# The first mixer's share of the second block's output projection, moved in among the other mixers

## The chip, the cores and the metric

The kernel runs as one launch on one core of a Trainium2 chip. The metric is the device time of that launch in microseconds, the median of three runs.

## The reference

Two blocks follow each other on the same 512 x 1024 tensor x, all in float32. The change touches only the second block, which has two layers. One layer computes:

```
h = rms_norm(x, norm_g[l, 0]) * (1 + sc1) + sh1
aq, ak, av, bq, bff, bfb, bi, bg, cq, ck, cv = split(h @ w_in[l])
o_a = mixer_a(aq, ak, av)            # full attention, 6 heads of 64: 384 columns
o_b = mixer_b(bq, bff, bfb, bi, bg)  # gated linear scan, both directions, 4 heads: 256 columns
o_c = mixer_c(cq, ck, cv)            # attention with a fixed bias, 6 heads: 384 columns
x = x + g1 * (concat(o_a, o_b, o_c) @ w_out[l])
h = rms_norm(x, norm_g[l, 1]) * (1 + sc2) + sh2
x = x + g2 * conv_ffn(h)
```

`w_out` is 1024 x 1024. Its first 384 rows meet o_a alone, so that part of the product needs only mixer a.

## The kernel before, in words

Everything is held transposed: tiles of 128 features by 512 positions. A float32 product is made of three matmuls in a rounded format (`mm3`, line 178): every operand is split into a high and a low part (`hi`, a ScalarE cast, line 141; `lo`, a VectorE subtraction, line 146), and high times high, low times high and high times low are summed in PSUM. `wload` (line 151) brings a weight tile in: a DMA into one of two raw buffers, one cast for up to 1024 columns, one subtraction per 512 columns, into one of two pairs wh, wl.

A layer of block 2 (`block2`, line 1728) writes x to DRAM (xd, eight tiles of 128 x 512), runs the mixers, reloads x, and does the output projection in eight tiles n (`residual`, line 1719: matmuls into a PSUM tile dn, then one VectorE instruction x = dn * gate + x). Each tile has 8 feature steps k of three matmuls. The tiles n = 0 to 2 are done for all 512 columns at once, n = 3 to 7 first for columns 0 to 255 and later for 256 to 511. In between stands the first half of the norm in front of the FFN (`norm_halves`): squares, their sum, a column sum on TensorE, a reciprocal root on GpSimd, rows on TensorE, then the scaled halves hh and hl. The FFN's first matmuls (up) use that first half.

The mixers are Python generators, each yielding a cost at the end of a step. `weave` (line 1617) takes several such streams with a weight each and always continues the one with the smallest cost divided by weight. The third weave of a layer has three streams: mixer b's second head pair (four projections, then `b_levels`, its scan by nine doubling distances, then output and norm); the twelve half-heads of mixer c (`c_units`, line 1425); and a chain of mixer b's first output, two `c_prep` (line 1392: a projection, its norm and the split of the queries that later heads of c need), norms, two gate projections (`b_gate`) and `room`. `room` (line 1285) sends the mixers' finished outputs through `mix_done` (line 1275), which splits them into tiles oh, ol. These stand in a pool of 24 buffers (`hblk`, line 511), which hold the projections' input hh, hl (16 of them) and the attention tiles E as well.

The order in which the generators emit is a priority, not the final order: the framework's scheduler simulates the engines and puts into each engine's queue, among what is ready, what was emitted first. Each engine, and SP's queue of DMA issues, then runs its queue strictly in that order. PSUM tiles of the tag mm (three banks) serve the projections, the levels and dn.

Of the kernel before, what the change touches and what calls it, by code (L numbers as in the profile page):

```python
# [13 lines left out]
ALU = mybir.AluOpType  # L14
AX = mybir.AxisListType

P = 128
D = 1024
KD = D // P
S = 512  # L20
# [83 lines left out]
class Kern:  # L104
# [1527 lines left out]
                s[2] += c  # L1632
                held = []

    def mixers(self):
        nc = self.nc
        self.gn = self.cp.tile([P, 1], F32, tag="gb2", name=self.nm("gb2"))
        nc.sync.dma_start(self.gn, self.A["gb_2"][self.l])
        self.gc = self.cp.tile([P, 2], F32, tag="gc2", name=self.nm("gc2"))
        nc.sync.dma_start(self.gc, self.A["gc_2"][self.l])  # L1640
        nc.vector.tensor_scalar(self.gc[:, 0:1], self.gc[:, 0:1], 0.125, None, op0=ALU.mult)
        self.cqs, self.cks = [], []
        self.full, self.wait = True, []
        self.oh, self.ol, self.y2, self.bz, self.cn, self.bst, self.bav = {}, {}, {}, {}, {}, {}, {}
        self.zz = [self.bp.tile([P, 2, S], F32, tag="zz", name=self.nm("zz"), bufs=2) for _ in range(2)]
        for z in self.zz:
            nc.gpsimd.memset(z[64:P, 0], 0.0)
            nc.gpsimd.memset(z[0:64, 1], 0.0)
        self.weave((self.b_prep(0), 8.0), (self.a_prep(), 25.5))
        self.weave((self.b_levels(0), 7.0), (self.a_units(), 31), (self.stagger(self.c_prep([3]), self.c_prep([0]), self.c_vals()), 20.0))  # L1650
        if 1:
            for i in (0, 1, 2):
                self.mix_done(i, self.y2[i])
            self.weave((self.chain(self.b_prep(1), self.b_levels(1), self.b_out(1), self.b_norm(1)), 40.0), (self.c_units(), 22.0),
                       (self.chain(self.b_out(0), self.stagger(self.c_prep([1]), self.b_norm(0), self.c_prep([2]), self.b_gate(1), self.b_gate(0)), self.room()), 28.0))
            self.b_done(0)
            self.b_done(1)

# [69 lines left out]
    def block2(self):  # L1728
        nc, tc, A, F = self.nc, self.tc, self.A, self.fill
        self.stat, self.ptb, self.halves = [("s", 2), ("pt", 2)], 2, 0  # L1730
        self.psum = lambda tn, name="mm": self.ps1(name)
        self.bw = {"t": S}
        self.cp = self.ctx.enter_context(tc.tile_pool(name="cp2", bufs=1, reuse_waits="tile"))
        self.ind64 = self.const("ind64", [P, 2])
        self.lmask = self.const("lmask", [P, 5, 32]).bitcast(I32)

        lbr = self.const("b_lb", [P, 2, 2, 2])
        e = self.cp.tile([P, 3, 2, 2, 2], F32, tag="lbe", name="lbe")[:, 0]
        mx = self.cp.tile([P, 2, 2], F32, tag="lbm", name="lbm")
        nc.vector.tensor_tensor(mx, lbr[:, :, 0, :], lbr[:, :, 1, :], op=ALU.max)  # L1740
        for l in range(2):
            nc.vector.tensor_tensor(e[:, :, l, :], lbr[:, :, l, :], mx, op=ALU.subtract)
        nc.scalar.activation(e, e, AF.Exp)
        nc.vector.tensor_tensor(mx, e[:, :, 0, :], e[:, :, 1, :], op=ALU.add)
        rc = self.cp.tile([P, 2, 2], F32, tag="lbr", name="lbr")
        nc.vector.reciprocal(rc, mx)
        self.lb = self.cp.tile([P, 2, 2, 2], F32, tag="lb", name="lb")
        self.oml = self.cp.tile([P, 2, 2, 2], F32, tag="oml", name="oml")
        for l in range(2):
            nc.vector.tensor_tensor(e[:, :, l, :], e[:, :, l, :], rc, op=ALU.mult)  # L1750
        nc.vector.tensor_tensor(self.lb[:, :, 0, :], e[:, :, 0, :], e[:, :, 0, :], op=ALU.subtract)
        nc.vector.tensor_tensor(mx, e[:, :, 0, :], e[:, :, 1, :], op=ALU.add)
        nc.vector.tensor_tensor(self.lb[:, :, 1, :], mx, e[:, :, 0, :], op=ALU.subtract)
        nc.vector.tensor_scalar(self.oml, self.lb, -1.0, 1.0, op0=ALU.mult, op1=ALU.add)
        self.g1 = self.gains("ng1", A["norm_g_2"][1, 0])
        for l in range(2):
            self.l = l
            with ExitStack() as lay:
                g2 = self.gains("ng2", A["norm_g_2"][l, 1])
                mod = self.ada[l][0]  # L1760
                xd = self.dram([KD, P, S], f"xm{l}")
                with self.pool(f"bq{l}", bufs=1, side="right") as bq, self.pool(f"bpm{l}", bufs=1) as bp:
                    self.bp = self.ptp = Pools(bp, bq, 'f2,t,rot,va2,qa,bz,pT'.split(","))
                    self.bb = dict(t=4, rx=1, rot=4, qa=6, ka=6, y=7, bz=2, f=1, yz=2, ex=2)
                    for n in range(KD):
                        nc.sync.dma_start(xd[n], self.x[n])
                    self.mixers()
                    bq.tile([P, 56], F32, tag="pad", name=f"pad{l}")
                    oy = [self.oh[i] for i in range(8)], [self.ol[i] for i in range(8)]
                    self.x = []  # L1770
                    self.x = []
                    for n in range(KD):
                        x = self.hblk(F32, "x")
                        nc.sync.dma_start(x, xd[n])
                        self.x.append(x)
                    ks = [(k, k) for k in (0, 1, 2, 5, 6, 3, 4, 7)]
                    late = []
                    for n in range(KD):
                        w = self.wload(A["w_out_2"][l, n], KD, P)
                        if n < KD - 5:  # L1780
                            self.residual(n, [(w, oy, ks)], (0, S), mod[:, 16 + n, 0:1])
                        else:
                            self.residual(n, [(w, oy, ks)], (0, 256), mod[:, 16 + n, 0:1])
                            late.append(w)
                with tc.tile_pool(name=f"bpf{l}", bufs=1, reuse_waits="tile") as self.bp:
                    self.bb = dict(t=5, act=44, mw=2, w3=2)
                    parts = self.norm_halves(mod, g2, 3, 4, lambda: self.b2("act"))
                    F.add(next(parts))
                    F.drain()
                    for n in [*range(KD - 2, KD), *range(KD - 5, KD - 2)]:  # L1790
                        w = late[n - KD + 5] if n >= KD - 2 else self.wload(A["w_out_2"][l, n], KD, P)
                        self.residual(n, [(w, oy, ks)], (256, S), mod[:, 16 + n, 0:1])
                    F.add(next(parts))
                    F.drain()
                    self.halves = 2
                    self.ffn(mod)
        for n in range(KD):
            nc.sync.dma_start(A["outT"][n], self.x[n])
# [114 lines left out]
```

## Time and profile before

| | |
|---|---|
| median of 3 runs | 3018.26 us (3018.15 to 3021.32) |
| the profiled execution | 3018.07 us, span 3016.3 us |
| TensorE busy | 2910.5 us, 96% of the span |
| VectorE busy | 1921.0 us, 64% |
| ScalarE busy | 1351.2 us, 45% |
| GpSimd busy | 249.8 us, 8% |
| DMA through SP's queue | 328.81 MB, 32.9% of 16 engines' span |

Times in the profile are microseconds from the start of the span. PE is TensorE's matmuls, PEld its weight loads, DVE is VectorE, ACT is ScalarE, POOL is GpSimd, SPq is SP's queue of DMA issues. A matmul's busy time is a modelled one and overlaps that of the next; its pace is read from start to start. PEclk is the granted TensorE clock as a share of 2.4 GHz; the levels are 2.4 and 1.2 GHz, so a value between is a mixture over time. An arrow in square brackets says how long an engine had stood idle before an instruction, and what ended that.

### The profile page before, as it was taken

To read this page: it belongs to the slowest core of one execution; us is meant where nothing else is said; L and a number is where in the kernel's file an instruction comes from. 1 tells how busy PE (TensorE), PEld (TensorE's weight loads), DVE (VectorE), ACT (ScalarE), POOL (GpSimd) and SP (SyncE) were. 2 spreads that over 40 slices of the span, in tenths; PEclk is the share of its full clock that TensorE was granted. 3 is DMA by queue.
4 is the path that set the end of the run, shared out by engine and by line. 5 is a ranking of instruction groups with operands and counts; after the bars stand their busy time and mean duration, and the time that the engine had idled before them with its cause. 6 is when DMAs were issued, how large, how long until landed. Compare 5 with 4: busy or idle time off the path is not lost.

```text
span 3016.3 us, 46253 instructions
## 1 busy us (share of the span) xinstructions
PE 2910.5 (96%) x17942; PEld 2415.4 (80%) x17942; DVE 1921.0 (64%) x3731; ACT 1351.2 (45%) x2417; POOL 249.8 (8%) x492
## 2 busy tenths in 40 slices
PE   7999999999998999999999999999999998999999
PEld 5888888888887888777778776788888876788887
DVE  5565655555556566665666777688853788576642
ACT  3445454322235345653225675544433676454421
POOL 0000000001112000000112222000000223000000
PEclk9999999999998999999999998999999999999999
DMA  6221111333342323124664211355543311232233
GB/s 228 87 67 60 48 63 64 121 127 120 119 161 84 125 83 107 52 69 169 222 216 134 70 50 47 99 175 196 203 144 109 103 43 60 79 105 98 98 102 95
DMA packets 113164, 331.77 MB, mean 110 GB/s; under 512 B 18160, under 2 KB 20720, under 8 KB 112944
## 3 DMA queue, kind: packets, MB, share of 16 engines
q1 hardware_dynamic: 112944, 328.81, 32.9%
q8 instruction: 141, 2.31, 0.3%
q14 instruction: 79, 0.65, 0.1%
HBM read 300.51 MB, written 17.76 MB: 106 GB/s over the span
## 4 chain that ended last, share of the span: by engine, by line
PE 83%; DVE 8%; ACT 2%; issue 1%; DMA 1%; POOL 1%; SPq 0%; DVEq 0%; ACTq 0%; POOLq 0%
PE mm L186 31%; PE up L186 15%; PE dn L186 10%; PE pu L186 5%; PE pv L600 4%; PE pt L595 4%; PE po L186 3%; PE s L907 2%; PE pre L186 1%; PE s L624 1%; PE s L1267 1%; DVE zz L1571 1%; DVE wl L146 1%; PE pq L186 1%; DVE E L607 1%
## 5 line engine op out<-in xcount | busy, mean ns | idle before, releaser
L146 DVE TENSOR_TENSOR wl<-wraw,wh 128x512 fp32r<-128x512 f32 x704 | 472.4, 710 | 389.2 <-ACT wh L141 385.7
L141 ACT CAST wh<-wraw 128x1024 fp32r<-128x1024 f32 (+4 forms) x363 | 364.9, 1005 | 741.0 <-PE mm L186 227.4
L186 PE MATMUL mm<-hh,wh 128*128 128x512 f32 (+1 forms) x1232 | 483.5, 396 | 11.1 <-ACT wh L141 4.0
L186 PE MATMUL mm<-hl,wh 128*128 128x512 f32 (+1 forms) x1232 | 486.1, 395 | 0.0
L186 PE MATMUL mm<-hh,wl 128*128 128x512 f32 (+1 forms) x1232 | 484.9, 394 | 0.2
L186 PEld LDWEIGHTS mm<-hh,wh 128*128 128x128 f32 x1232 | 233.5, 191 | 59.8 <-ACT wh L141 6.7
L186 PEld LDWEIGHTS mm<-hh,wl 128*128 128x128 f32 x1232 | 234.4, 190 | 49.3 <-DVE wl L146 3.0
L186 PEld LDWEIGHTS mm<-hl,wh 128*128 128x128 f32 x1232 | 234.8, 191 | 46.8 <-issue 2.9
L186 PE MATMUL up<-hh,wh 128*128 128x512 f32 (+1 forms) x688 | 260.8, 381 | 3.4 <-ACT wh L141 2.1
L186 PE MATMUL up<-hh,wl 128*128 128x512 f32 (+1 forms) x688 | 261.1, 380 | 0.2 <-DVE wl L146 0.2
L186 PE MATMUL up<-hl,wh 128*128 128x512 f32 (+1 forms) x688 | 260.7, 380 | 0.5 <-DVE hl L352 0.2
L597 ACT COPY pT<-pt 128x512 f32<-128x512 f32 (+1 forms) x304 | 158.8, 551 | 176.6 <-PE pt L595 175.3
L283 DVE SCALAR_TENSOR_TENSOR macc<-mw,sc,macc 128x1024 f32<-128x1024 f32 x140 | 181.7, 1313 | 70.7 <-DMA mw<-w_mod 37.5
L595 PE MATMUL pt<-ident,E 128*128 128x128 f32 x1120 | 174.6, 282 | 4.7 <-DVE E L607 4.2
L595 PEld LDWEIGHTS pt<-ident,E 128*128 128x128 f32 x1120 | 127.2, 141 | 37.3 <-issue 25.7
L186 PEld LDWEIGHTS up<-hh,wh 128*128 128x128 f32 x688 | 128.9, 188 | 29.1 <-ACT wh L141 2.5
L186 PEld LDWEIGHTS up<-hl,wh 128*128 128x128 f32 x688 | 129.1, 188 | 26.3 <-DVE hl L352 1.1
L186 PEld LDWEIGHTS up<-hh,wl 128*128 128x128 f32 x688 | 129.2, 188 | 25.5 <-issue 0.8
L1020 POOL TENSOR_TENSOR m<-m,gt 128x768 f32<-128x768 f32 (+1 forms) x32 | 55.1, 1721 | 1084.3 <-DVE gt L1016 755.6
L186 PE MATMUL mm<-ch,wh 128*128 128x256 f32 x496 | 141.8, 286 | 0.1
L186 PE MATMUL mm<-ch,wl 128*128 128x256 f32 x496 | 141.6, 286 | 0.0
L186 PE MATMUL mm<-cl,wh 128*128 128x256 f32 x496 | 141.3, 285 | 0.0
(442 smaller groups left out, 6129.6 us busy)
## 6 DMA issues: line engine op xcount, KB each, us to landing
wraw<-w_in SPq DMA_DIRECT2D x158, 512.0 KB, 3.5
mw<-w_ada SPq DMA_DIRECT2D x96, 512.0 KB, 4.3
wraw<-w_up SPq DMA_DIRECT2D x88, 512.0 KB, 3.5
mw<-w_mod SPq DMA_DIRECT2D x32, 512.0 KB, 3.6
wraw<-w_down SPq DMA_DIRECT2D x32, 512.0 KB, 3.5
wraw<-w_branch SPq DMA_DIRECT2D x24, 512.0 KB, 4.0
wraw<-w_out SPq DMA_DIRECT2D x22, 512.0 KB, 3.4
wraw<-w_o SPq DMA_DIRECT2D x19, 512.0 KB, 4.2
```

Source lines behind the costliest of these rows:

```text
L141: self.nc.scalar.copy(out, in_)
L146: (eng or self.nc.vector).tensor_tensor(out, in_, hi.bitcast(F32), op=ALU.subtract)
L186: self.last = self.nc.tensor.matmul(ps[: n1 - n0, c0 - o:c1 - o], lhsT=a[:, k, n0:n1], rhs=b[j][:, c0:c1], start=start and i == 0, stop=st ...
L283: nc.vector.scalar_tensor_tensor(acc[r], w, sc[:, k, r:r + 1], acc[r], op0=ALU.mult, op1=ALU.add)
L595: nc.tensor.transpose(pt[:, o * P:o * P + P], ecol(j, kb), self.ident)
L597: nc.scalar.copy(tt[:, :n], pt[:, :n])
L600: nc.tensor.matmul(pv[64 * j:64 * j + 64, :P], lhsT=vst(kb), rhs=tt[:, o * P:o * P + P], start=i == ends[j][0], stop=i == ends[j][-1])
L607: self.nc.vector.tensor_scalar(e, e, r, None, op0=ALU.mult)
L624: nc.tensor.matmul(s[:, c0:c1], lhsT=q[:, i * P:(i + 1) * P], rhs=kp[:, a0:a0 + c1 - c0], start=pi == 0, stop=pi == 1)
L907: self.nc.tensor.matmul(ps, lhsT=a[:96, i * P:(i + 1) * P], rhs=b[:96, c0:c1], start=pi == 0, stop=pi == 2)
L1020: nc.gpsimd.tensor_tensor(ms[n][:, :tn], ms[n][:, :tn], m[:, :tn], op=ALU.add)
L1267: nc.tensor.matmul(s, lhsT=q[:, i * P:(i + 1) * P], rhs=kp, start=pi == 0, stop=pi == 1)
```

## The change

A new generator, `w_out_a`, computes for each of the eight tiles n the part of the output projection that belongs to mixer a (k = 0, 1, 2), multiplies it by the gate, adds it to that tile of x from DRAM and writes the tile back. It is emitted at the end of the third stream, behind `room`, and that stream's weight goes from 28 to 45. The projection behind the mixers then covers the five other steps, in the order 5, 6, 3, 4, 7, with weight tiles of 640 columns instead of 1024.

```
+    def w_out_a(self, xd, mod):
+        nc = self.nc
+        oy = [self.oh[i] for i in range(3)], [self.ol[i] for i in range(3)]
+        for n in range(KD):
+            x = self.b2("t", name="xa")
+            nc.sync.dma_start(x, xd[n])
+            w = self.wload(self.A["w_out_2"][self.l, n][:, :3 * P], 3, P)
+            ps = self.ps1("dn")
+            self.mm3(ps, w, oy, [(0, S)])
+            nc.vector.scalar_tensor_tensor(x, ps, mod[:, 16 + n, 0:1], x, op0=ALU.mult, op1=ALU.add)
+            nc.sync.dma_start(xd[n], x)
+            yield 2.1
+
-    def mixers(self):
+    def mixers(self, xd, mod):
...
-                       (self.chain(self.b_out(0), self.stagger(self.c_prep([1]), self.b_norm(0), self.c_prep([2]), self.b_gate(1), self.b_gate(0)), self.room()), 28.0))
+                       (self.chain(self.b_out(0), self.stagger(self.c_prep([1]), self.b_norm(0), self.c_prep([2]), self.b_gate(1), self.b_gate(0)), self.room(), self.w_out_a(xd, mod)), 45.0))
...
-                    ks = [(k, k) for k in (0, 1, 2, 5, 6, 3, 4, 7)]
+                    ks = [(k - 3, k) for k in (5, 6, 3, 4, 7)]
...
-                        w = self.wload(A["w_out_2"][l, n], KD, P)
+                        w = self.wload(A["w_out_2"][l, n][:, 3 * P:], 5, P)
...
-                        w = late[n - KD + 5] if n >= KD - 2 else self.wload(A["w_out_2"][l, n], KD, P)
+                        w = late[n - KD + 5] if n >= KD - 2 else self.wload(A["w_out_2"][l, n][:, 3 * P:], 5, P)
```

## Rows read from the trace of the kernel before

**Rows 1.** The page: busy time of the engines over the span.
```profile
PE 2910.5 (96%) x17942; PEld 2415.4 (80%) x17942; DVE 1921.0 (64%) x3731; ACT 1351.2 (45%) x2417; POOL 249.8 (8%) x492
```

**Rows 2.** Table by stage, layer 0: length, busy us by engine, clock, DMA share, GB/s.
```profile
1776.00:1818.00 42.00, 42.00 (x266) 33.92 (x266) 26.63 (x65) 32.78 (x52) 3.44 (x3) 1.00 0.25 76
1818.00:1882.00 64.00, 58.64 (x525) 42.36 (x524) 51.14 (x122) 36.65 (x78) 22.18 (x43) 0.84 0.14 46
1882.00:1920.00 38.00, 33.74 (x250) 24.24 (x249) 23.95 (x66) 20.62 (x43) 3.05 (x11) 1.00 0.24 73
1920.00:1949.00 29.00, 28.93 (x186) 25.94 (x187) 15.82 (x30) 13.80 (x27) 0.00 (x0) 0.94 0.33 110
1949.00:1961.00 12.00, 12.00 (x103) 12.00 (x102) 8.59 (x19) 7.47 (x14) 2.96 (x11) 1.00 0.40 131
1961.00:1980.00 19.00, 17.09 (x130) 15.70 (x129) 12.96 (x31) 9.10 (x21) 2.18 (x11) 1.00 0.44 140
```

**Rows 3.** The same table, layer 1.
```profile
2516.00:2566.00 50.00, 40.33 (x470) 30.22 (x466) 45.65 (x97) 31.55 (x64) 17.58 (x33) 0.93 0.12 41
2566.00:2606.00 40.00, 36.22 (x215) 24.22 (x216) 20.66 (x57) 18.24 (x39) 2.56 (x11) 0.96 0.21 68
```

**Rows 4.** Timeline of PE, layer 0, output projection: start, us, instruction.
```profile
1930.94 0.39 PE L186 MATMUL dn<-ol,wh 128*128 128x512 f32 x1
1931.17 0.39 PE L186 MATMUL dn<-oh,wl 128*128 128x512 f32 x1
...
1934.11 0.28 PE L186 MATMUL dn<-ol,wh 128*128 128x256 f32 x1
1934.23 0.28 PE L186 MATMUL dn<-oh,wl 128*128 128x256 f32 x1
```

**Rows 5.** Groups by form, 1920 to 1980: count, busy us, mean ns, idle before.
```profile
L186 PE MATMUL dn<-oh,wh 128*128 128x256 f32 x80 | 22.5, 283 | 0.0
...
L186 PE MATMUL dn<-oh,wh 128*128 128x512 f32 x14 | 6.1, 449 | 1.9 <-ACT oh L141 1.9
```

**Rows 6.** Timeline of PE, layer 0, the first projection step behind the mixers.
```profile
1919.88 0.73 PE L186 MATMUL dn<-oh,wh 128*128 128x512 f32 x2 [1.86 <-ACT oh L141]
```

**Rows 7.** DMA issues by line: count, KB each, median us to landing.
```profile
wraw<-w_down SPq DMA_DIRECT2D x16, 384.0 KB, 3.0
...
x<-xm SPq DMA_DIRECT2D x16, 256.0 KB, 2.8
```

**Rows 8.** Groups by form over the span: casts, subtractions, x additions.
```profile
L146 DVE TENSOR_TENSOR wl<-wraw,wh 128x512 fp32r<-128x512 f32 x670 | 458.6, 723 | 386.3 <-ACT wh L141 382.9 <-PE pk L186 1.6
...
L1726 DVE SCALAR_TENSOR_TENSOR x<-dn,ada,x 128x512 f32<-128x512 f32 x21 | 15.8, 750 | 46.1 <-PE dn L186 46.1
...
L141 ACT CAST wh<-wraw 128x768 fp32r<-128x768 f32 x18 | 15.0, 835 | 52.8 <-PE dn L186 36.5 <-issue 16.3
...
L146 DVE TENSOR_TENSOR wl<-wraw,wh 128x256 fp32r<-128x256 f32 x26 | 10.9, 420 | 1.5 <-ACT wh L141 1.4
```

**Rows 9.** Timeline of ACT, layer 0, a weight cast in the projection's first half.
```profile
1938.06 1.05 ACT L141 CAST wh<-wraw 128x1024 fp32r<-128x1024 f32 x1 [1.46 <-DMA wraw<-w_out]
```

**Rows 10.** Timelines of DVE and PE: last first-half addition, first up matmul.
```profile
1949.31 0.48 DVE L1726 SCALAR_TENSOR_TENSOR x<-dn,ada,x 128x256 f32<-128x256 f32 x1 [0.29 <-PE dn L186]
...
1961.29 0.28 PE L186 MATMUL up<-hh,wh 128*128 128x256 f32 x1
```

**Rows 11.** Timeline of DVE, layer 0: query splits and score evaluations of mixer c.
```profile
1859.25 1.40 DVE L146 TENSOR_TENSOR qa<-nc,qa 64x512 fp32r<-64x512 f32 x2
...
1879.01 0.68 DVE L1438 CUSTOM_DVE_ANT_0 E<-s,tb 128x512 f32<-128x512 f32 x1
...
1889.73 1.40 DVE L146 TENSOR_TENSOR qa<-nc,qa 64x512 fp32r<-64x512 f32 x2
...
1894.30 0.69 DVE L1438 CUSTOM_DVE_ANT_0 E<-s,tb 128x512 f32<-128x512 f32 x1 [3.18 <-PE s L1267]
```

**Rows 12.** Groups by form, 1818 to 1882: GpSimd's running sums of the levels.
```profile
L1530 POOL TENSOR_TENSOR f<-f 128x512 f32<-128x512 f32 x6 | 7.3, 1211 | 26.2 <-DVE sm L1445 21.5 <-DVE ey L1523 4.7
```

**Rows 13.** Timeline of ACT, layer 0: the first casts of mixer outputs.
```profile
1894.80 1.64 ACT L141 CAST oh<-y 128x512 fp32r<-128x512 f32 x3
```

More of the change, by code (lines that the diff above doesn't have):

```diff
@@ L1766, in block2 @@
                         nc.sync.dma_start(xd[n], self.x[n])
-                    self.mixers()
+                    self.mixers(xd, mod)
                     bq.tile([P, 56], F32, tag="pad", name=f"pad{l}")
```

## The prediction

> **What bounds the kernel now.** Read first the page's busy line: TensorE is busy 96% of the span [rows 1], so only a stretch where it stands or runs slowly can give time back. Next the table by stage for layer 0 of the second block [rows 2]: the last weave is the stretch from 1776 to 1920 us, the output projection runs from 1920 to 1961, the first FFN matmuls from 1961 to 1980. The reader is to see three regimes in the weave. From 1776 to 1818 TensorE is full at clock 1.00 while VectorE has 15.4 us free: the projections set the pace. From 1818 to 1882 it turns round: VectorE is busy 51 of 64 us, TensorE stands 5.4 us and its granted clock averages 0.84, a mixture of the 2.4 and the 1.2 GHz level after waits. From 1882 to 1920 both have holes. Layer 1 shows the same shape [rows 3]: VectorE 45.65 of 50 us, TensorE standing 9.7 us, clock 0.93. Behind the mixers TensorE is full again.
>
> So the free TensorE time lies in the weave: in layer 0, 64 x (1 - 0.84) = 10.2 us by clock, 5.4 + 4.3 us standing, 20 us in all; in layer 1, 50 x 0.07 + 9.7 + 40 x 0.04 + 3.8 = 18.6 us. These are floors, since a modelled busy time covers small gaps. But half of it lies where VectorE is nearly full.
>
> **The change, part by part.** Times are against the profiled execution's own 3018.07 us (span 3016.3 and 1.8 around it), 0.2 us under the median of the runs.
>
> Matmuls. A 512-column step costs 0.23 us and a 256-column one 0.12 us, start to start [rows 4]. Before, a layer has 72 of the first and 240 of the second. The rows by form find 14 of each of three kinds at 512 columns and 80 of each at 256 between 1920 and 1980 [rows 5]; with the 2 that start at 1919.88 [rows 6] 44 of the 72 stand behind the mixers, and 28 (6.4 us) have run as fill among the c heads. So behind the mixers stand 44 x 0.23 + 240 x 0.12 = 38.9 us. After, there are 8 x 9 = 72 at 512 columns in the weave (16.6 us), and behind it 3 x 15 x 0.23 + 5 x 2 x 15 x 0.12 = 28.4 us. Of those, k = 5 and 6 of three tiles (18 x 0.23 = 4.1 us) can still run as fill, since the three mm banks allow it, which leaves 24.3. The stretch behind the mixers loses **14.6 us** per layer, and the weave gains 16.6 + 4.1 - 6.4 = 14.3: total TensorE work stays. The gain is only what the weave's free 19 to 20 us swallow.
>
> What is late next behind the mixers? First, the weights. A tile with half the columns takes TensorE 2.88 us now and 1.8 us after. The cycle of a raw buffer is landing, cast, subtraction. 320 KB land in about 2.9 us (256 KB 2.8, 384 KB 3.0 [rows 7]); the cast of 640 lies below the 0.84 us of 768 columns, say 0.73, and the subtractions at 0.69 + 0.3 follow from 512 and 256 columns [rows 8]. With 0.3 for queueing that is 4.9 us for two tiles, 2.45 each against 1.8. Already today a cast stands 1.46 us for its DMA [rows 9]. Four tiles are not loaded ahead: 4 x 0.65 = 2.6 us, of which I take 2, since second-half work of tile 6 fits into the gaps. Second, the norm chain. From the last addition to the first half (1949.31) to the first up matmul (1961.29) are 12.0 us [rows 10], hidden now by second-half matmuls. After, these are 9.0 us, so TensorE stands 3 us; two come back because the second norm then starts earlier against the up stage, which today stands 1.9 us of 19 [rows 2]. Net 1 us. So 14.6 - 2 - 1 = **11.6 us** gained behind the mixers, bounds 6.6 (the chain eats the second halves' 45 x 0.12 = 5.4 and the weights 2.6) and 14.6.
>
> Added in the weave. VectorE: eight subtractions of 384 columns (between 0.42 and 0.72, say 0.55) and eight x additions of 512 at 0.75 [rows 8]: 10.4 us. ScalarE: eight casts of 384, about 0.5 (under the 0.84 of 768), 4 us, beside its 27 us free between 1818 and 1882; nothing on the path. DMA: per layer eight loads of x, eight stores and eight weight loads of 192 KB, 24 issues; the DMA engines are busy 14% there [rows 2], and each landing (under 3 us [rows 7]) lies ahead of a 2 us group: nothing. On SP's queue a store waits for its addition, and the next weight or c-bias load stands behind it. That can stretch a group from 2.1 us towards 0.75 + 2.8 + 1.1 us, which eight groups over 60 us bear. The later reload of x waits for the last store, and x is needed only at the first addition behind the mixers. PSUM: a dn tile holds an mm bank that the levels also use, two of three stay.
>
> The extra VectorE time cannot be hidden where that engine is full, but 15.4 us are free ahead of 1818 and 14 behind 1882. Of the 10.4 us I put half, 5.2, on the path to the last c head. Bounds of the shift of the weave's end: the whole 16.6 us of matmuls, if nothing fits; and below nothing, from the weights.
>
> The weights of the streams. The third stream was 28 for 27.8 us of cost; now 45 for 44.6, so its steps come 1.6 times sooner in the order against the levels and the c heads. The rows say that this matters: the query splits of c tiles end at 1860.65 and 1891.13, and c scores are evaluated at 1894.30 behind the second [rows 11]: the last four of the twelve c units cannot begin before their c_prep. Earlier c_prep lets them run in holes. Against that the gate projections come, in the order, ahead of most levels and push these back. The two are of one size; I take 0, with -4 (a quarter of the 15 us between 1879 and 1894 without a c score, at layer 0) as the lower end.
>
> Shift +5.2, gain 11.6: -6.4 us per layer, two layers -12.8. I add 1.2 us for the clock, which the fill should keep at its upper level for some of the 10.2 us lost today: -14, **3004 us**.
>
> A rule against it: POOL's running sums over f take 1.21 us on average in the full stretch [rows 12], with VectorE at 80%, and they feed the level chain. By the Trainium skill, "SBUF — State Buffer", section "Who interferes with whom", a VectorE operation with two SBUF inputs holds off a GpSimd operation that reads SBUF for its whole length. The eight new subtractions are of that kind; each meeting a POOL operation would add at most 0.55 us, 4.4 per layer, and the sum would be 3013 by that page. No row here shows a POOL operation doubled, and POOL is busy 22 of 64 us, so the sum goes without it.
>
> **Rivals.**
> (1) VectorE becomes the bound and the kernel gets slower. Place: the levels and c units between 1818 and 1882. All 10.4 us land on the path, and each of the eight additions, in VectorE's order, stands for its matmul group while exponent and mask work queues behind; today the 512-column additions wait 46.1 us for 21, 2.2 each [rows 8]. At 1 us each: shift 18.4, against 11.6: +6.8 per layer, 3032. It decides from a shift of 11.6 on. For it: 51 of 64 and 45.65 of 50 us busy. Against: the free time on both sides.
> (2) The order is the larger part: the c units are no longer gated, fill takes all free TensorE time, the end of the weave moves 4 us ahead: -15.6 per layer, 2987. For it: the gap in rows 11. Against: the last c units still follow each other through two score banks.
> (3) Given back behind the mixers: weights and norm chain take 8 of the 14.6, 6.6 stays, shift 5.2: -1.4 per layer, 3015. For it rows 9 and 10.
> (4) It does not do what it says: oh tiles share 24 buffers with the projections' input, and the first oh cast comes only at 1894.80 today [rows 13]. If the last projection stays late, the 16.6 us run in the tail, whose holes take about 7: shift 9.6, -2 per layer, 3014. Against: the higher weight moves that projection ahead.
>
> **How the numbers follow.** Forecast 0.47, (1) 0.22, (2) 0.12, (3) 0.12, (4) 0.07. The likeliest case alone spans 2994 to 3012 (shift 0.5 to 9). The range is 2988 to 3027: it leaves out half of (1) and half of (2) and holds the rest. 0.2% is 6 us, about what a measurement tells from no change: under 3012 faster, over 3024 slower. Faster: most of the forecast, (2), a little of (3) and (4): 0.61; same 0.18; slower 0.21.
>
> **What would show it.** Right: dn matmuls with oh of the first three tiles between the levels, clock near 1.00 in the weave's middle, VectorE some 10 us more there; the weave's end up to 9 us later against its start; first-half additions under 2.5 us apart; up matmuls about 12 us behind the last of them with TensorE standing. Wrong: the end of the weave more than 11.6 us later, or the moved matmuls bunched behind the last c head, or an x load that waits for the store of another tile.

## The result, and the profile after

The changed kernel takes 3042.78 us (median of 6 runs, 3037.56 to 3044.85), the kernel before 3018.2 in the same sets of runs: ratio 1.0077, 95% interval 1.0064 to 1.0090. It is slower by 24.6 us, where 3004 was forecast. The profiled execution has a span of 3041.4 us.

The page's busy line answers to [rows 1]. TensorE's work has hardly changed (2910.5 to 2912.9 us), so what was added is time in which it stands:

```profile
PE 2912.9 (96%) x17852; PEld 2409.7 (79%) x17852; DVE 1930.9 (63%) x3763; ACT 1356.4 (45%) x2433; POOL 252.9 (8%) x492
```

The table by stage for layer 0 answers to [rows 2], with the middle stretch cut at 1846. The columns are: length, then busy us of PE, PEld, DVE, ACT and POOL, the granted clock, the DMA share, GB/s. After the change:

```profile
1776.00:1818.00 42.00, 42.00 (x259) 34.25 (x258) 27.39 (x67) 32.07 (x51) 3.42 (x3) 1.00 0.23 68
1818.00:1846.00 28.00, 28.00 (x209) 20.52 (x207) 15.76 (x45) 12.88 (x28) 3.43 (x16) 1.00 0.18 55
1846.00:1882.00 36.00, 27.14 (x345) 19.40 (x346) 34.99 (x75) 20.31 (x43) 15.94 (x26) 0.91 0.20 62
1882.00:1920.00 38.00, 34.69 (x187) 23.06 (x184) 23.09 (x51) 19.75 (x39) 5.38 (x13) 1.00 0.33 111
1920.00:1940.00 20.00, 12.68 (x103) 8.59 (x102) 10.54 (x33) 8.79 (x21) 0.00 (x0) 0.90 0.46 153
```

The same middle of the kernel before:

```profile
1818.00:1846.00 28.00, 25.49 (x299) 17.86 (x297) 23.74 (x58) 14.87 (x32) 7.73 (x14) 0.82 0.17 53
1846.00:1882.00 36.00, 33.15 (x227) 24.50 (x228) 27.40 (x65) 21.77 (x46) 14.45 (x29) 0.85 0.12 40
```

The reader is to see two engines that worked side by side taking turns. Before, VectorE is busy 23.7 of 28 and 27.4 of 36 us. After, it is nearly half idle (15.8 of 28) while TensorE is full, then full (35.0 of 36) while TensorE stands 8.9 us. Then the tail: TensorE stands 3.3 us from 1882 to 1920 and 7.3 from 1920 to 1940. Before, it stood 4.3 us in the first of these stretches, and the second was already the output projection.

What fills TensorE first is seen in its groups by form between 1814 and 1846 (busy us, mean ns, idle before). Before, four distances of the level chain and 13 matmuls of projections:

```profile
L1503 PE MATMUL lv<-zz,Y 128*32 128x64 f32 x128 | 3.5, 267 | 0.1
L186 PE MATMUL mm<-hh,wh 128*128 128x512 f32 x5 | 2.4, 472 | 0.0
L186 PE MATMUL mm<-hl,wh 128*128 128x512 f32 x4 | 1.6, 390 | 0.0
L186 PE MATMUL mm<-hh,wl 128*128 128x512 f32 x4 | 1.6, 389 | 0.0
```

After, 60 matmuls of projections, and of the levels only what stands ahead of the first distance (kk, which both kernels have):

```profile
L186 PE MATMUL mm<-hl,wh 128*128 128x512 f32 x20 | 8.0, 400 | 0.0
L186 PE MATMUL mm<-hh,wh 128*128 128x512 f32 x20 | 7.9, 396 | 0.0
L186 PE MATMUL mm<-hh,wl 128*128 128x512 f32 x20 | 7.9, 395 | 0.0
L1503 PE MATMUL lv<-zz,kk 128*32 128x64 f32 x28 | 0.6, 222 | 0.0
```

Most of those are the two gate projections (48 matmuls in all). ScalarE reads them out (bz) at 1819.53 and 1842.73, before at 1854.62 and 1885.17. The first tile of the level chain (cd) now follows the second of them; before, it stood ahead of both. ScalarE's timeline after:

```profile
1819.53 0.59 ACT L1602 ACTIVATE bz<-mm 128x512 f32<-128x512 f32 x1
...
1842.73 0.59 ACT L1602 ACTIVATE bz<-mm 128x512 f32<-128x512 f32 x1
...
1847.05 0.37 ACT L1510 COPY cd<-lv 128x256 f32<-128x256 f32 x1
```

and before:

```profile
1825.09 0.37 ACT L1510 COPY cd<-lv 128x256 f32<-128x256 f32 x1
...
1854.62 0.60 ACT L1602 ACTIVATE bz<-mm 128x512 f32<-128x512 f32 x1
...
1885.17 0.59 ACT L1602 ACTIVATE bz<-mm 128x512 f32<-128x512 f32 x1
```

On VectorE, the first score of the last four c units (before at 1894.30 [rows 11]) is evaluated at 1912.92. It stands behind the new x additions, and each of those waits for its matmuls (in brackets):

```profile
1903.24 0.75 DVE L1645 SCALAR_TENSOR_TENSOR xa<-dn,ada,xa 128x512 f32<-128x512 f32 x1 [6.80 <-PE dn L186]
...
1907.75 0.75 DVE L1645 SCALAR_TENSOR_TENSOR xa<-dn,ada,xa 128x512 f32<-128x512 f32 x1 [3.28 <-PE dn L186]
...
1912.92 0.68 DVE L1438 CUSTOM_DVE_ANT_0 E<-s,tb 128x512 f32<-128x512 f32 x1
```

Two landmarks on TensorE bound what lies behind the mixers: the first projection step behind the last oh cast (answers to [rows 6]) and the first up matmul (answers to [rows 10]).

```profile
1940.45 1.22 PE L186 MATMUL dn<-oh,wh 128*128 128x512 f32 x2 [1.86 <-ACT oh L141]
...
1974.77 0.58 PE L186 MATMUL up<-hh,wh 128*128 128x256 f32 x1 [2.20 <-ACT hh L351]
```

From first to second are 34.3 us, before 41.4, so 7.1 are gained there (8.6 in layer 1). The first landmark lies 20.6 us later (19.3 in layer 1, the delay carried over from layer 0 taken off). That is the result: a shift of 20 against a gain of 8 per layer.

### The profile page after: what moved, and what is told of

Its sections match the earlier page's. It is cut to its first block, busy times and chain, and to the rows that moved or that the text cites. A ratio compares the mean times of both kernels' runs of the same rounds, so it can differ in the third digit from the quotient of the medians.

```text
span 3041.4 us, 46227 instructions
## 1 busy us (share of the span) xinstructions
PE 2912.9 (96%) x17852; PEld 2409.7 (79%) x17852; DVE 1930.9 (63%) x3763; ACT 1356.4 (45%) x2433; POOL 252.9 (8%) x492
## 4 chain that ended last, share of the span: by engine, by line
PE 81%; DVE 7%; issue 5%; ACT 2%; POOL 1%; DMA 1%; SPq 0%; DVEq 0%; ACTq 0%; POOLq 0%
PE mm L186 31%; PE up L186 16%; PE dn L186 8%; PE pu L186 5%; PE pv L600 4%; PE pt L595 3%; PE po L186 3%; PE s L907 2%; PE pre L186 1%; PE s L624 1%; DVE zz L1571 1%; PE s L1267 1%; DVE wl L146 1%; PE pq L186 1%; DVE E L607 1%
## 5 line engine op out<-in xcount | busy, mean ns | idle before, releaser
L146 DVE TENSOR_TENSOR wl<-wraw,wh 128x512 fp32r<-128x512 f32 (+1 forms) x720 | 471.7, 694 | 379.4 <-ACT wh L141 376.7
L141 ACT CAST wh<-wraw 128x1024 fp32r<-128x1024 f32 (+5 forms) x379 | 366.6, 967 | 725.9 <-PE mm L186 227.3
```

The lines of the kernel that those rows point to most:

```text
L141: self.nc.scalar.copy(out, in_)
L146: (eng or self.nc.vector).tensor_tensor(out, in_, hi.bitcast(F32), op=ALU.subtract)
```

## The experiments

Ratios are to the kernel before, with 95% intervals. Each set of runs timed the kernel before anew (medians 3015.25 to 3017.86 us), so small differences between runs of different sets are read from the ratios. The "second distance" is the VectorE multiplication zz<-bq,ez with which the level chain's second doubling distance begins; in the kernel before it starts at 1823.31. Theory O: the stream weight reorders the work, and that is the loss. Theory V: VectorE, in its fixed order, stands for the moved groups.

**The weight alone** (kernel before)

```
-  ... self.room()), 28.0))
+  ... self.room()), 45.0))
```

> The kernel before with the third stream's weight at 45 and nothing else. Theory O (order): the weight alone pushes four projections ahead of the levels, whose second distance then starts about 20 us later, as after the change (1847 instead of 1823), and the weave ends 8 to 12 us later per layer: 3034 to 3042. Theory V (VectorE's order): without the eight additions nothing stands, the earlier c_prep even helps: 3010 to 3020.

Measured: 3042.45 us, 1.0081 (1.0069 to 1.0093). Without a single moved matmul a loss of the same size is there (24.9 us). VectorE has its hole and its full stretch again, and the c score that I had put down to the x additions is just as late (1911.13). Theory V falls as the main cause.

```profile
1818.00:1846.00 28.00, 28.00 (x203) 20.45 (x205) 15.45 (x44) 14.16 (x29) 2.61 (x11) 1.00 0.23 71
1846.00:1882.00 36.00, 24.81 (x320) 17.93 (x308) 35.24 (x78) 20.27 (x40) 15.96 (x30) 0.86 0.10 32
```

**The moved work alone** (changed kernel, weight 28)

```
-  ... self.room(), self.w_out_a(xd, mod)), 45.0))
+  ... self.room(), self.w_out_a(xd, mod)), 28.0))
```

> The changed kernel with the third stream's weight back at 28; the moved matmuls stay. Theory O: the second distance starts near 1825 again, the weave's end moves by 8 us against before instead of 20, and with the 7 us gained behind the mixers the time is 3016 to 3022. Theory V: the additions stand all the same and queue the last c units behind them: 3038 to 3046.

Measured: 3015.97, 0.9991 (0.9982 to 1.0000): the move itself is worth nothing that can be told from no change. The second distance is back (1823.81), and the last oh cast comes at 1927.92, 9.2 us after that of before. The moved matmuls now run in the tail, and TensorE, which stood 4.3 us of these 38 before [rows 2], is full there:

```profile
1882.00:1920.00 38.00, 38.00 (x248) 28.19 (x247) 28.79 (x72) 20.71 (x45) 3.04 (x11) 1.00 0.43 139
```

**The x addition off VectorE** (weight 45, then 28)

```
-  nc.vector.scalar_tensor_tensor(x, ps, mod[:, 16 + n, 0:1], x, op0=ALU.mult, op1=ALU.add)
+  t = self.b2("t", name="xg")
+  nc.scalar.activation(t, ps, AF.Copy, scale=mod[:, 16 + n, 0:1])
+  nc.gpsimd.tensor_tensor(x, x, t, op=ALU.add)
```

> The changed kernel, weight 45, but the addition to x is taken from VectorE: ScalarE copies the product times the gate out of PSUM, GpSimd adds it to x. Theory V: the c scores computed at 1879 are evaluated at once and not at 1912.9, the shift falls by some 10 us per layer: 3018 to 3026. Theory O: the levels stay 24 us late, only the additions' own 6 us of VectorE go, half of it on the path: 3036 to 3041.

> The changed kernel with weight 28, and the addition to x taken from VectorE (ScalarE copies out of PSUM times the gate, GpSimd adds). At weight 28 the shift is still some 8 us per layer. If VectorE's share of it is what the prediction said (half of its added 10.4 us), taking 6 of the 10.4 away gives back 3 us per layer: 3010. If the shift is only TensorE's work that found no hole, nothing changes: 3016.

Measured at 45: 3034.05, 1.0053 (1.0041 to 1.0065), 8.7 us less than the changed kernel by the medians and 7 by the ratios, though the c score stays at 1912.17. At 28: 3017.7, 1.0009 (1.0000 to 1.0018), no gain over 3015.97. So the added x additions cost something at weight 45 and nothing at 28. They do not cost it in the stretch where VectorE is full: in layer 0 seven of the eight stand behind 1882, where VectorE is busy 23.1 of 38 us, and there they wait for their matmul groups, up to 6.80 us. At 28 the longest such wait is 1.28 us. What comes back at 45 in layer 0 comes back behind the c score: the last oh cast is 4.6 us sooner (1934.69 instead of 1939.26).

**The projection behind the mixers by itself** (weight 28; mixer a's share is left out altogether)

```
-  ... self.room(), self.w_out_a(xd, mod)), 45.0))
+  ... self.room()), 28.0))
```

> Only the shortened projection behind the mixers (five steps per tile, weight tiles of 640 columns), weight 28; mixer a's share of the projection is left out altogether. It measures the gain behind the mixers by itself. By the prediction's term of 11.6 us per layer: 2995. By what the changed kernel's landmarks show (34.4 instead of 41.4 us from the last mixer output to the first up matmul, 7 us per layer): 3004.

Measured: 2999.56, 0.9937 (0.9925 to 0.9949), 18.0 us or 9.0 per layer: between the two expectations. Its stretch from the last first-half addition to the first up matmul nearly keeps its length (13.05 us, before 13.66) and has TensorE standing 3.0 us in it:

```profile
1942.43:1955.48 13.05, 10.05 (x79) 9.27 (x77) 9.42 (x23) 8.91 (x21) 3.07 (x11) 1.00 0.38 123
```

**Which projections: c_prep, then gates** (kernel before). First c_prep at the place of 45 and the gates, with `room` behind them, at that of 28; then the complement:

```
+  (self.chain(self.scaled(self.chain(self.b_out(0), self.stagger(self.c_prep([1]), self.b_norm(0), self.c_prep([2]))), 28 / 45),
+              self.pad(6.65), self.b_gate(1), self.b_gate(0), self.room()), 28.0)
```

```
+  (self.chain(self.b_out(0), self.stagger(self.c_prep([1]), self.b_norm(0), self.c_prep([2]))), 28.0),
+  (self.chain(self.pad(17.6), self.b_gate(1), self.b_gate(0), self.room()), 45.0)
```

`scaled` multiplies the yielded costs, `pad` yields one cost and does nothing.

> The kernel before, but the first output of mixer b and the two c_prep stand where weight 45 puts them, while the two gate projections and room stand where 28 puts them. If the gate projections are what costs (theory O in its narrow form: two of them ran between 1814 and 1843 with the first level's matmuls behind them on TensorE), this costs nothing: 3010 to 3020. If any projection pulled ahead costs the same, half of the 24 us come back: 3028 to 3036.

> The kernel before with the complement of the c_prep experiment: both c_prep stand where 28 puts them, the two gate projections and room where 45 puts them, nothing moved. If the gate projections ahead of the levels are the whole cost of the weight: 3036 to 3046. If they cost only together with early c_prep: 3016 to 3026.

Measured: early c_prep 3015.39, 0.9998 (0.9989 to 1.0007); early gates 3043.48, 1.0089 (1.0075 to 1.0102). The two gate projections, with `room` behind them, are the whole cost of the weight. `room` moved along in both runs and was not tried by itself. In the second run its first oh cast comes at 1860.17, when the second distance is already late (1847.01), so it does not delay that; but four of its splits then stand in VectorE's full stretch and not behind it, 3.6 us in layer 0, where 13 are lost per layer. Early gates, by stage:

```profile
1818.00:1846.00 28.00, 28.00 (x250) 20.75 (x250) 14.94 (x45) 14.03 (x29) 5.42 (x22) 1.00 0.23 73
1846.00:1882.00 36.00, 21.28 (x268) 15.16 (x267) 34.43 (x74) 19.07 (x39) 11.97 (x19) 0.78 0.13 40
```

**Other weights** (changed kernel, 22 and 34)

> The changed kernel with the third stream's weight at 22, below the 28 of before. Theory O: later gate projections lie beside more of the levels, and the time falls a little further, 3006 to 3014; but the moved matmuls come later too and bunch behind the last c head, which makes 3016 to 3024. Theory V has no say.

> The changed kernel with the third stream's weight at 34, between 28 (3016) and 45 (3043). If the gate projections change places with the levels one by one, it lies between: 3022 to 3034, with the second distance between 1824 and 1847. If there is one switch (one gate projection that goes ahead of the first level's matmuls or does not), it is 3016 or 3043.

Measured: 22 gives 3055.1, 1.0134 (1.0118 to 1.0150); 34 gives 3030.61, 1.0039 (1.0025 to 1.0053). At 34 one gate is read out at 1831.84 and the other at 1886.55, with the second distance at 1839.36: the projections pass the levels one by one. My expectation for 22 was wrong both ways. Its second distance is early (1822.55), but now the last queries are split only at 1902.94, and the last c units wait for that; their first score is 11.4 us later than at 28 (1893.49). The loss against 28 is 19.6 us per layer; the rest of it was not taken apart.

```profile
1902.94 1.40 DVE L146 TENSOR_TENSOR qa<-nc,qa 64x512 fp32r<-64x512 f32 x2 [0.69 <-ACT qa L141]
1904.93 0.69 DVE L1438 CUSTOM_DVE_ANT_0 E<-s,tb 128x512 f32<-128x512 f32 x1 [0.60 <-PE s L1267]
```

**All of the moved part off VectorE** (weight 28; the addition as above, and the subtraction on GpSimd)

```
+  self.lo(l[:, a:e], raw[:, a:e], h[:, a:e], nc.gpsimd)
```

> As the last but one, and the eight subtractions of 384 columns go to GpSimd too: the moved part now costs VectorE nothing. If VectorE's 10.4 us are half on the path: 3006. If the shift is TensorE's alone: 3016. A GpSimd subtraction stands at the head of the level chain's running sums, so up to 3 us worse is possible.

Measured: 3021.31, 1.0025 (1.0014 to 1.0035). It gets worse, not better; the last section shows what may make it so. With nothing of the moved work on VectorE the shift is still there, so at weight 28 VectorE's added instructions are not what makes it.

**The moved work among the levels.** Weight 28; mixer a's outputs are split into buffers that stand idle here, so the moved work need not wait for `room`, and it is a stream of its own:

```
+  spare = [self.b2("ka", F32R, "oh") for _ in range(2)] + [self.b2("rot", F32R, "oh") for _ in range(2)]
+  spare.append(self.bp.tile([P, S], F32R, tag="va2", name=self.nm("oh"), bufs=2))
+  spare.append(self.hblk(F32R, "oh"))
...
+  (self.chain(self.pad(21.0), self.w_out_a(xd, mod)), 42.0)
```

The second adds the eviction from above; the third has the pad at 8.4 and the weight at 28.

> The third stream at 28, and mixer a's outputs are split into five buffers that stand idle in this weave (two of ka, two of rot, one of va2) and one of the 24, so the moved matmuls no longer wait for the last projection; they are a stream of their own among the levels (their costs reach from 0.5 to 0.9 of the weave's measure). Theory H (holes): at weight 28 they ran from 1900 on, behind 1893, where TensorE is nearly full anyway; among the levels, where it stands 5.4 us and runs at 0.84, they cost half as much, shift 4 instead of 8 us per layer: 3008. Theory F (the levels' stretch is full on VectorE): additions and subtractions push the levels, shift 8 to 12: 3016 to 3026.

> As the last, with the addition to x on GpSimd behind a ScalarE copy out of PSUM instead of on VectorE. Theory H: no different from the last one, or 3 us less, 3005 to 3008. Theory F: 4 to 8 us less than the last one.

> As the one but last (addition on VectorE), but spread thinner and sooner: from 0.3 to 0.9 of the measure. Theory H: 3006 to 3012. If what runs ahead of the levels delays them as the gate projections did at weight 45, it is later: every 0.23 us matmul ahead of the second distance costs its time, up to 5 us per layer: 3018 to 3026.

Measured: 3036.95, 1.0065 (1.0053 to 1.0078); 3041.69, 1.0082 (1.0068 to 1.0096); 3032.41, 1.0049 (1.0037 to 1.0062). Theory H, mine, falls. F named the direction, but neither the size nor the reason: with the additions off VectorE it is no better. The second distance is as late as at weight 45 (1849.86 in the first). When the level chain's first matmuls run at last, three tiles are just being read out of PSUM: the squares of c_prep, mixer b's values and the first moved group. TensorE, ScalarE and VectorE:

```profile
1848.55 0.65 PE L1503 MATMUL lv<-zz,kk 128*32 128x64 f32 x32
```

```profile
1846.21 0.60 ACT L1321 ACTIVATE sq<-mm 128x512 f32<-128x512 f32 x1
1846.69 0.59 ACT L1248 COPY vf<-mm 128x512 f32<-128x512 f32 x1
```

```profile
1849.20 0.75 DVE L1649 SCALAR_TENSOR_TENSOR xa<-dn,ada,xa 128x512 f32<-128x512 f32 x1 [0.29 <-DMA xa<-xm]
```

That is as many as there are mm banks, so banks became a suspect. It was tested at the two weights, not in these three kernels.

**Parked tiles out of PSUM sooner** (weight 45; weight 28; the kernel before). The copy of mixer b's values and the squares of the last two c_prep get idle buffers instead of t:

```
-  f = self.b2('t', name="vf")
+  f = self.b2(buf, name="vf")                       # "ka" for mixer b's second pair
...
-  r = self.stats([p])
+  r = self.stats([p], {1: "ka", 2: "rot"}.get(i, "t"))
```

> The changed kernel, weight 45; the copy of mixer b's values and the squares of the last two c_prep go to idle buffers of ka and rot instead of t. In the kernel before and in the changed one these two wait some 30 us for a t buffer, and each keeps one of the three mm banks of PSUM that long. Theory B (banks): the levels are late because gate projections and parked banks leave them none; freed, the second distance starts near 1830 and the time is 3020 to 3030. Theory O (order on TensorE): the levels still stand behind the gate projections in the queue, 3040 to 3046.

> The same buffers with weight 28. Theory B: levels with three banks instead of one between 1817 and 1843 run 3 to 5 us sooner per layer, 3006 to 3012. Theory O: the levels are paced by VectorE and their own chain, 3014 to 3018.

> The kernel before with the same buffers and nothing moved: what these buffers give by themselves. Theory B: 3008 to 3014. Theory O: 3015 to 3020.

Measured: 3040.36, 1.0078 (1.0065 to 1.0092); 3012.19, 0.9988 (0.9979 to 0.9997); 3011.27, 0.9979 (0.9971 to 0.9988). At weight 45 the values leave PSUM at 1826.18 instead of 1847.32, but the second distance still comes only at 1840.80 (1847.13 without these buffers, near 1830 by theory B), and the ratio is that of the changed kernel (1.0077): the parked banks aren't the cause there. In the kernel before the buffers are worth 5 us by themselves, and with them it beats both kernels.

**Put together** (early c_prep, gates at the place of 28, idle buffers; with and without the moved work)

> All that has not cost anything, put together with the moved work: c_prep at 45's place, gates and moved work at 28's, idle buffers for the parked tiles. Theory O: 3008 to 3013, no more than the idle buffers give. If early c_prep makes room for the moved work in the tail: 3000 to 3007.

> The same without the moved work: the kernel before with c_prep at 45's place and the idle buffers. Theory O: 3008 to 3013, the same as with the moved work, since that only carries matmuls from a full stretch to a nearly full one.

Measured: 3021.3, 1.0017 (1.0008 to 1.0026), and 3011.64, 0.9986 (0.9977 to 0.9994). Here the moved work costs 9.7 us, against my expectation of none. In layer 0 its last oh cast comes 14.1 us later, of which 4.0 are there at the last c score, so 10 arise behind it:

```profile
1928.15 1.66 ACT L141 CAST oh<-y 128x512 fp32r<-128x512 f32 x3 [3.08 <-DVE y L603]
```

```profile
1914.04 1.66 ACT L141 CAST oh<-y 128x512 fp32r<-128x512 f32 x3 [1.38 <-DVE y L603]
```

The traces say what stands there: between 1909 and 1928 TensorE runs 53 matmuls of the output projection among those of the last c heads, 12 us at 0.23. They are the last moved groups, and behind them first steps of the projection proper. Without the moved work such steps have run before 1905, and from there to 1914 TensorE has none of them and waits 2.6 us for ScalarE and VectorE. So the moved work lengthens a tail that had too few holes for it. Another order there was not tried.

## Why the prediction was wrong

The failed step is the last term of the weave, "The two are of one size; I take 0" for the stream weights. Both halves had been seen: c_prep sooner, gates ahead of the levels. The first is worth nothing (0.9998). The second costs 24.9 us (weight alone) to 26.9 us (gates and `room` alone), 12 to 13 per layer. I priced the gain of the first at 4 us from a gap in the c scores and put the second equal to it without working it out. The rows for it were there: [rows 2] has TensorE full until 1818 with VectorE 15 us free. Projections put ahead of the levels only lengthen that stretch (after the change it runs to 1846, with VectorE busy 15.8 of the last 28 us). The levels that they push back are VectorE's work, and fall into a stretch that is 80% full of it already. The two projections are 48 matmuls at 0.23, 11 us of TensorE per layer, taken from beside the levels and put ahead of them. That is an estimate, and it gives the order of the loss; that the order is the cause is shown by the two runs that part c_prep from the gates.

The other terms, per layer, by the landmarks on TensorE and ScalarE:

- Shift without the weight, forecast 5.2. At weight 28 the last oh cast is 9.2 and 6.2 us later in the two layers, less 0.5 and 1.6 carried in: 8.7 and 4.6, mean 6.7. The number is near by luck, for the reason was another. The forecast put half of VectorE's added 10.4 us on the path; taking 6 of these off VectorE, and then all, gained nothing (1.0009 and 1.0025 against 0.9991). What the run shows instead is a tail in which TensorE is full (38.00 of 38 us): the moved matmuls that find no hole lengthen it.
- Gain behind the mixers, forecast 11.6. Measured 9.0 by itself, 7.1 and 8.6 in the changed kernel. The weight feed was nearly right (TensorE waits 1.3 us for wh and wl in layer 0, 2 forecast). The norm chain was not: I took 1 us. I had read 1949.31 in [rows 10] as the last first-half addition, but three tiles of 512 and five of 256 are eight, and the eighth stands at 1947.63; 1949.31 is the first of the second halves. The chain is thus 13.66 us long, stays 13.0 after the change, and the 5.4 us of shortened second halves, which run beside it, come back as some 0.6. That is the chain's part of the lower bound that the prediction named, nearly in full.
- Durations were right: subtraction 0.55 (0.55 forecast), cast 0.51 (0.5), addition 0.75. The additions wait 23.2 us in 16 for their groups, 1.45 each, more than rival (1) gave them.
- Clock, forecast 0.6: nothing. Its mean is 0.983, before 0.984. Between 1846 and 1882 it is 0.91 with TensorE standing; the slow share only changed its place.

The eighth addition, which [rows 10] leaves out, on VectorE in the kernel before:

```profile
1947.63 0.48 DVE L1726 SCALAR_TENSOR_TENSOR x<-dn,ada,x 128x256 f32<-128x256 f32 x1 [2.67 <-PE dn L186]
```

The sum, per layer: 13.4 for the weight (changed kernel against the same at 28, 26.8 over two layers), 3.7 for the gain, 1.5 for the shift, 0.6 for the clock are 19.2; the forecast missed by 38.8 over two layers, 19.4.

Of the rivals, (1) had the nearest time (3032) and the right place, a VectorE that becomes the bound, but in the main the wrong reason: not its added instructions, but its old ones, pushed together. The weight alone loses as much without the added ones; in the changed kernel the x additions, as waits in VectorE's order, are worth 7 to 9 of the 24.6. (2) had the right cause with the wrong sign. (3), 3015, is close to what the move does at weight 28 (gain 7.6 and 8.2 in the two layers, mean shift 6.7). (4) is seen at 28 as well: the oh casts start at 1893.99 and the moved matmuls run in the tail. Of the Trainium skill's rule on VectorE and GpSimd, which the prediction cites, nothing shows in the averages: GpSimd's sums over f take 1.23 us (1.05 to 1.48) between 1846 and 1900, most of it with VectorE full, before 1.21 (1.06 to 1.58) [rows 12].

The Trainium skill says in "Perfetto Trace Analysis", section "Optimization Strategy", that where the most-contended engine changes over time, interleaving the regimes may help. This case's tables agree, in the other direction: the weight undid such an interleaving, and 12 us a layer is what it had been worth.

## What to carry to other kernels

Matmuls whose inputs are long ready are a stock to be spent beside the other engine's work; a priority that spends them early looks free, since TensorE stays full, and the bill comes when the other engine's chain runs alone. Where a change has a main part and a small constant, price the constant by what it moves past what, and run each alone first: here the constant was the whole loss. Count the instructions of a phase before naming its last one.

## What the runs showed of the hardware

A VectorE instruction took longer beside GpSimd's. In the kernel with the moved subtractions and additions on GpSimd, the c heads' normalisation E<-E,sm, in layer 0 between 1818 and 1935, takes up to 1.50 us; in the kernel before it takes 0.48 to 0.49 in that stretch. After (min/median/max in ns):

```profile
L607 DVE TENSOR_SCALAR E<-E,sm x24: 473/482/1502, 1822.7 to 1923.5; 128x512 f32<-128x512 f32 x24
```

Before:

```profile
L607 DVE TENSOR_SCALAR E<-E,sm x24: 477/482/489, 1817.8 to 1914.8; 128x512 f32<-128x512 f32 x24
```

One pair of them, usually 0.88, takes 2.65 us from 1912.56 on, and GpSimd's two operations beside it span 1912.04 to 1914.92 (a second pair, at 1917.61, takes 2.42):

```profile
1912.56 2.65 DVE L607 TENSOR_SCALAR E<-E,sm 128x512 f32<-128x512 f32 x2
```

```profile
1912.04 1.46 POOL L146 TENSOR_TENSOR wl<-wraw,wh 128x384 fp32r<-128x384 f32 x1
1913.46 1.46 POOL L1647 TENSOR_TENSOR xa<-xa,xg 128x512 f32<-128x512 f32 x1
```

The Trainium skill, "SBUF — State Buffer", section "Who interferes with whom", says that a VectorE operation with one SBUF input, when it runs in a mode that uses both ports (which it names as possible for this kind), and a GpSimd operation exclude each other, and that the one issued first holds the ports for its whole length. These rows agree, with VectorE as the one that waits. It need not be: at 1922.93 a GpSimd subtraction takes 1.85 us (the shortest of its kind takes 0.99), and the VectorE pair beside it 0.87.

The two long pairs add 3.3 us in layer 0. This kernel is 3.6 us slower by the medians than the one of the same set with only the additions on GpSimd (3017.7), and 5.3 slower than the changed kernel at weight 28 of another set. Whether the long pairs make that difference wasn't measured by itself.
